# HGRN2 heads of a two-layer backbone: the context's state moved behind the sixth decay level, that level's scores in 32-wide strips

## The chip, the cores and the metric

The kernel runs on one core of a Trainium2 chip. Its engines work side by side, each with a queue of its own, in order: TensorE (PE for the matmuls, PEld for its weight loads), VectorE (DVE), ScalarE (ACT), GpSimd (POOL) and SyncE (SP, which here issues most loads). The metric is the device time of one execution in microseconds, the median of several; all times below are in us unless marked otherwise.

## The reference

Two layers act on 1024 latent tokens of width 1024 and a prefix of 256 context tokens. Layer 0 joins neighbourhood attention and a chunked mLSTM. Layer 1, which the change touches, is sixteen bidirectional HGRN2 heads (a gated linear recurrence), key and value width 128:

```
f = lb + (1 - lb) * sigmoid(f_pre)          # decay, per token and key channel, one per direction
S_t = diag(f_t) S_{t-1} + (1 - f_t) v_t^T   # state, 128 x 128
o_t = silu(q_t) S_t                         # both directions added
S_0 = state of the same recurrence over the 256 context tokens
y = rms_norm(o) * silu(z);  out = x + gate * (y @ w_out)
```

All is fp32. The context matters in layer 1 only through S_0: for each direction the sum over context tokens of v times k, k decayed by the product of all later f.

## The kernel before, in words

**Numbers.** A matmul of fp32 values is made of three matmuls of rounded halves: `dense` (L131 to L133) issues high x high, high x low and low x high for each 128-deep slice.

**Stages.** Layer 0 takes the time up to about 2165, with layer 1's first projections at its end (`hg_wide`, for the first head). Then come the sixteen heads, one every 60.3 us, until about 3110, then the output projection. Sixteen heads share one code path: `hg_intra`, `hg_close`, `hg_states`, `hg_chain`, `hg_scan`, and `hg_vt` and `hg_proj` for the next head.

**One head's scores.** The products q_t k_s with all decays between s and t are built in seven levels (`hg_level`): level `lev` pairs neighbouring blocks of 1 << lev tokens. K and Q hold keys and queries decayed to the border of their block, F (gF) the block's total decay. At each level ACT copies the keys of each left or right block side by side (ksel, L1467, one buffer), DVE multiplies K by the totals (L1462), PE multiplies ksel against Q in strips (L1431, 32 wide in levels 0 to 4, 64 wide in levels 5 and 6), DVE updates Q (L1462 again, same line), picks the strips into the diagonal blocks D (copy_predicated, L1491; levels 0 to 4) and halves the table of totals (L1489). Levels 5 and 6 are copied to the score matrix A (gA) by ACT (L1495, L1499). The strips of a level need the Q update of the level before and this level's ksel; ksel needs the K update of the level before.

**What PE does between levels.** `hg_vz` is a generator that gives the value and gate projections in eight pieces of 24 matmuls, 128x256 (2.65 us each); one piece runs after each level's strips, two after the last. After every second piece ACT copies the values out, makes a sigmoid, and DVE multiplies (gz, L1342).

**The context.** `hg_ctx` makes S_0: DVE scans the products of f over the context in both directions (L1354, L1355, into E, tile gEc), makes 1 - f (L1356) and the product k (L1357); PE transposes k (L1362, four), ACT copies it (L1365, tile gknc), PE multiplies it with the values (L1372, four), DVE copies the two states out (L1378). It is called at level 3, its second half at level 4.

**The previous head's tail.** `prev(1)` and `prev(2)` (called at levels 1 and 2) run `hg_out` for the first and second half of the previous head's tokens: PE transposes A (L1584), ACT scales it into gyt, of which there is one buffer (L1589), POOL issues a store to yd (L1590); from head 8 on POOL also issues transfers that add gyt to sums in memory (`s`, L1595: one for the first half, three for the second). `prev(3)`, called at level 4, runs `sums`: `wo_sums` loads four quarters of the output weight (L1558, into tiles gknc and gEc), makes four subtractions on POOL (L1559) and stores four results (`sw`, L1565); `y_diff` (only where the previous head is 1 to 8) loads two halves of a y (L1571, L1572, again gknc and gEc), subtracts (L1573) and stores (L1575). wo_sums runs where the previous head is 0 to 13, so in heads 1 to 14.

**What sets the order.** The code is written for one stream; a scheduler with a timing model of its own then places each instruction in its engine's queue by the code's order, the data dependencies and priorities. `urgent()` lowers a priority value by a million, so that what stands inside goes first; `seg()` pins PE's segments one behind another; `issue_after(x)` keeps an instruction behind x. Within a queue nothing overtakes. A tile tag with one buffer makes the next user wait for all readers of the last.

Of the kernel before, what the change touches and what calls it, by code (L numbers as in the profile page):

```python
# [14 lines left out]
ALU = mybir.AluOpType  # L15
# [4 lines left out]
P = 128  # L20
# [25 lines left out]
class Prog:  # L46
# [874 lines left out]
    def out_y(self, tt, q, ysrc, yp, bufs, raws=None, tag="y", ks=((0, 4), (4, 4)), late=None):  # L921
        pl, tg, nb = raws or (yp, "wraw", self.yraws)
        hi, lo = [], []
        for k, n in ks:
            yh = self.t(yp, [P, 512], F32R, tag + "h", bufs)
            yl = self.t(yp, [P, 512], F32R, tag + "l", bufs)
            k0 = q * 8 + k
            if callable(ysrc):
                yr = ysrc(k0, tt)
            else:  # L930
                yr = self.t(pl, [P, 512], F32, tg, nb)
                self.nc.sync.dma_start(
                    out=yr[:, 0 : n * P].rearrange("p (j t) -> p j t", j=n),
                    in_=ysrc[k0 : k0 + n, :, tt * P : (tt + 1) * P].rearrange("j p t -> p j t"),
                )
            m = self.split(yh[:, 0 : n * P], yl[:, 0 : n * P], yr[:, 0 : n * P])
# [156 lines left out]
    def hg_wide(self, sp, s1, tp, x, ctx_part, early):  # L1093
        nc, a = self.nc, self.a
# [100 lines left out]
        def unit(u, kind, i):  # L1195
# [60 lines left out]
            def P4():  # L1256
                t["d"] = self.ps("x", [P, 512])
                prod(t["d"], form("P4"), (1, 1), True)
                if u == end:
                    last_part()  # L1260
                    finish(1, 0, t["u3"])

            def P6():
# [27 lines left out]
            def P3():  # L1291
                w = form("P3")
                prod(t["c"], w, 4, False)
                add(t["u2"], t["c"], t["u2"])
                finish(0, 1, t["u2"])
                cpart(1, w, 4, True)

# [48 lines left out]
    def hg_ctx(self, st, pool):  # L1346
        nc = self.nc
        Fc, v = st["Fc"], st["v"]
        E = self.t(pool, [P, 2, CTX], F32, "gEc", 1)
        k = self.t(pool, [P, 2, CTX], F32, "gq", 2)  # L1350
        nc.vector.memset(E[:, 0, CTX - 1 : CTX], 1.0)
        nc.vector.memset(E[:, 1, 0:1], 1.0)
        zz = self.zero[:, 0 : CTX - 1]
        nc.vector.tensor_tensor_scan(E[:, 0, 0 : CTX - 1][:, ::-1], Fc[:, 0, 1:CTX][:, ::-1], zz, 1.0, ALU.mult, ALU.add)  # L1354
        nc.vector.tensor_tensor_scan(E[:, 1, 1:CTX], Fc[:, 1, 0 : CTX - 1], zz, 1.0, ALU.mult, ALU.add)  # L1355
        nc.vector.tensor_scalar(out=k, in0=Fc, scalar1=-1.0, scalar2=1.0, op0=ALU.mult, op1=ALU.add)  # L1356
        nc.vector.tensor_tensor(out=k, in0=k, in1=E, op=ALU.mult)  # L1357
        p = self.ps("tr", [P, 4, P])
        with self.seg():
            for d in range(2):  # L1360
                for j in range(2):
                    m = nc.tensor.transpose(p[:, 2 * d + j, :], k[:, d, j * P : (j + 1) * P], self.ident)  # L1362
        self.last_pe = m
        kn = self.t(pool, [P, 4, P], F32, "gknc", 1)
        nc.scalar.copy(kn, p)  # L1365
        yield
        S = []
        u = self.ps("s", [P, 2, P])
        with self.seg():
            for d in range(2):  # L1370
                for j in range(2):
                    m = nc.tensor.matmul(  # L1372
                        u[:, d, :], lhsT=kn[:, 2 * d + j, :], rhs=v[:, 8 + j, :], start=(j == 0), stop=(j == 1)
                    )
        self.last_pe = m
        for d in range(2):
            s = self.t(pool, [P, P], F32, f"gS{d}", 8)
            nc.vector.tensor_copy(s, u[:, d, :])  # L1378
            S.append(s)
        yield S  # L1380


    def hg_intra(self, h, st, pool, prev):
# [27 lines left out]
        for lev in range(7):  # L1411
            if lev == 5:
                hv["A"] = self.t(pool, [P, 8, P], F32, "gA", 1)
            self.hg_level(hv, lev, pool)
            if lev in (1, 2) and prev:
                prev(lev)
            if lev == 3:
                ctx = self.hg_ctx(st, pool)
                next(ctx)
            if lev == 4:  # L1420
                S = next(ctx)
                if prev:
                    prev(3)
            next(tiles)
        next(tiles)
        return hv, S


    def strip(self, out, b, n, lhsT, rhs):
# [19 lines left out]
    def hg_level(self, H, lev, pool):  # L1449
# [3 lines left out]
        K, Q, A, D, Tt = H["K"], H["Q"], H.get("A"), H["D"], H["T"]  # L1453

        pick = lambda t: _skew(t[:, 0, :].rearrange("p (b s i) -> p b s i", s=2, i=h), 2, n)
        w = 32 if lev < 5 else 64
        out = self.ps("s", [P, 8, w])

        def update(t, o, step):
            v = bass.AP(t.tensor, t.offset, [list(t.ap[0]), [n + h, 2], [2 * h, nb], [1, h]])  # L1460
            tot = bass.AP(Tt.tensor, Tt.offset + o, [list(Tt.ap[0]), [step, 2], [2, nb], [0, h]])
            nc.vector.tensor_tensor(out=v, in0=v, in1=tot, op=ALU.mult)  # L1462

        with self.urgent():
            if lev < 6:
# [5 lines left out]
            for c, b in ((c, b) for c in range(8) for b in range(P // w)):  # L1471
                with self.seg():
                    o = c * P + b * w
                    r = out[:, c, :]
                    if lev < 6:
                        r = r.rearrange("p (b s i) -> p b s i", s=2, i=h)
                        lhsT, rhs = ksel[:, o : o + w], pick(Q)[:, o // (2 * h) : (o + w) // (2 * h)]
                    else:
                        lhsT = K[:, b, o : o + 64]
                        rhs = Q[:, 1 - b, c * P + (1 - b) * 64 : c * P + (2 - b) * 64]  # L1480
                    run = self.strip(r, b, w, lhsT, rhs)
            self.last_pe = run
            update(Q, n + 1, -n - 1)
            if lev == 6:
                update(K, 1, n - 1)
            Tv = Tt[:, :, 0 : 2 * nb].rearrange("p d (b s) -> p d b s", s=2)
# [3 lines left out]
        if lev < 5:  # L1490
            nc.vector.copy_predicated(D, self.lmask[:, lev + 1, :].unsqueeze(1).to_broadcast([P, 8, 32]), out)  # L1491
            return
        for b in range(2):
            s, e = slice(b * 64, (b + 1) * 64), slice((1 - b) * 64, (2 - b) * 64)
            nc.scalar.copy(A[s, :, s if lev == 5 else e], out[s])  # L1495
        if lev == 5:
            for b in range(4):
                s = slice(b * 32, (b + 1) * 32)
                nc.scalar.copy(A[s, :, s], D[s])  # L1499

    def hg_states(self, st, H, d, c0, c1):
# [99 lines left out]
    def build(self):  # L1601
        tc, nc, a = self.tc, self.nc, self.a
        dma = nc.sync.dma_start
        with ExitStack() as es:
# [226 lines left out]
            with tc.tile_pool(name="op0", bufs=2) as op, ExitStack() as wl:  # L1831
# [58 lines left out]
            with l1:  # L1890
# [41 lines left out]
                self.hg_vt(0, st, pool, wv)  # L1932
                prev = None
                for h in range(16):
                    hv, (Sf, Sb) = self.hg_intra(h, st, pool, prev)
# [374 lines left out]
```

## Time and profile before

| what | us |
|---|---|
| median of three runs | 3284.87 (3284.54 to 3287.74) |
| the profiled execution | 3282.71 |
| its span, first to last instruction | 3280.7 |
| PE busy | 3213.6 (98%) |
| DVE / ACT / POOL busy | 2183.9 (67%) / 1481.6 (45%) / 797.8 (24%) |
| mean granted TensorE clock | 0.998 |
| level 2 to level 5 strips of head 4 (starts) | 2419.32, 2423.32, 2427.43, 2432.04 |

The profiled execution's own time lies 2.0 us above its span. In a timeline row the first number is the start from the span's beginning, the second the duration, then engine, line, operation, out<-in with shapes, and in brackets the idle time just before, with what ended it. Operations on one engine are pipelined, so a start can lie a little before the end of the row above. Line numbers are those of the kernel before; in the changed kernel the same lines stand 2 to 6 further down (L1356 is L1358 there, L1431 is L1434, L1462 is L1465, L1489 is L1495, L1589 is L1593).

### The profile page before, as it was taken

How to read it: one execution, taken by the hardware profiler on the slowest of the kernel's cores; microseconds unless marked ns; L12 is line 12 of the kernel's file. 1: busy time of each engine (PE TensorE's matmuls, PEld its weight loads, DVE VectorE, ACT ScalarE, POOL GpSimd, SP SyncE). 2: the span in 40 equal slices, each digit the busy share in tenths (PEclk: the TensorE clock that was granted, in tenths of full speed). 3: DMA queues.
4: the chain of work that ended last, by engine and by line, in shares of the span. 5: the costliest groups of instructions: out<-in, count | busy, mean ns of one | idle time of the engine just before them, and what ended most of it. 6: DMA issues, size and time to landing. Idle time of an engine off the chain costs nothing.

```text
span 3280.7 us, 70941 instructions
## 1 busy us (share of the span) xinstructions
PE 3213.6 (98%) x27818; PEld 2864.3 (87%) x27818; DVE 2183.9 (67%) x4993; ACT 1481.6 (45%) x3460; POOL 797.8 (24%) x1191
## 2 busy tenths in 40 slices
PE   7999999999999999999999999999999999999999
PEld 6799899988989888888878788889999999999977
DVE  5846666666655456678766855577767777667766
ACT  5245554455544434445446433344444444444443
POOL 2222222222211112211110133312323323334210
PEclk9999999999999999999999999999999999999999
DMA  7713322232233434445564233332232333434376
GB/s 246 255 50 86 87 72 82 69 94 85 67 92 101 149 102 128 138 122 163 175 194 129 87 100 103 106 99 63 97 118 85 103 106 99 103 95 102 95 219 169
DMA packets 338126, 380.20 MB, mean 116 GB/s; under 512 B 34600, under 2 KB 269800, under 8 KB 336768
## 3 DMA queue, kind: packets, MB, share of 16 engines
q1 hardware_dynamic: 286032, 236.73, 24.5%
q0 software_dynamic: 51760, 138.94, 13.6%
q8 instruction: 219, 3.59, 0.5%
q14 instruction: 115, 0.94, 0.1%
HBM read 272.31 MB, written 103.08 MB: 114 GB/s over the span
## 4 chain that ended last, share of the span: by engine, by line
PE 80%; DVE 7%; DMA 6%; issue 4%; ACT 2%; POOL 1%; SPq 1%; DVEq 0%; ACTq 0%; POOLq 0%
PE mm L131 15%; PE mm L132 15%; PE mm L133 15%; PE acc L889 3%; PE tr L869 2%; PE s L1431 2%; PE x L131 2%; PE x L132 2%; PE x L133 2%; PE mm L951 2%; PE mm L953 2%; PE mm L952 2%; PE acc L661 2%; PE s L670 2%; PE s L1506 1%
## 5 line engine op out<-in xcount | busy, mean ns | idle before, releaser
L131 PE MATMUL mm<-wh,hh 128*128 128x256 f32 (+1 forms) x1440 | 446.0, 310 | 2.7 <-ACT wh L73 0.7
L132 PE MATMUL mm<-wl,hh 128*128 128x256 f32 (+1 forms) x1440 | 445.3, 309 | 0.0
L133 PE MATMUL mm<-wh,hl 128*128 128x256 f32 (+1 forms) x1440 | 442.7, 308 | 0.0
L131 PE MATMUL mm<-hh,wh 128*128 128x512 f32 (+1 forms) x1076 | 391.3, 364 | 1.8 <-ACT ev L399 0.7
L132 PE MATMUL mm<-hl,wh 128*128 128x512 f32 (+1 forms) x1076 | 387.4, 360 | 0.7 <-DVE hl L346 0.7
L133 PE MATMUL mm<-hh,wl 128*128 128x512 f32 (+1 forms) x1076 | 386.8, 360 | 0.0
L131 PE MATMUL mm<-wzh,hh 128*128 128x256 f32 x1024 | 295.7, 289 | 0.0
L131 PEld LDWEIGHTS mm<-wh,hh 128*128 128x128 f32 x1440 | 271.7, 189 | 17.1 <-issue 1.0
L132 PE MATMUL mm<-wzl,hh 128*128 128x256 f32 x1024 | 285.1, 278 | 0.0
L133 PE MATMUL mm<-wzh,hl 128*128 128x256 f32 x1024 | 284.9, 278 | 0.0
L132 PEld LDWEIGHTS mm<-wl,hh 128*128 128x128 f32 x1440 | 271.6, 189 | 12.6 <-issue 0.7
L133 PEld LDWEIGHTS mm<-wh,hl 128*128 128x128 f32 x1440 | 271.4, 188 | 11.8 <-issue 0.5
L131 PEld LDWEIGHTS mm<-hh,wh 128*128 128x128 f32 x1076 | 202.9, 189 | 31.5 <-ACT ev L399 2.8
L133 PEld LDWEIGHTS mm<-hh,wl 128*128 128x128 f32 x1076 | 202.4, 188 | 29.5 <-issue 0.2
L132 PEld LDWEIGHTS mm<-hl,wh 128*128 128x128 f32 x1076 | 202.9, 189 | 28.4 <-DVE hl L346 1.4
L131 PEld LDWEIGHTS mm<-wzh,hh 128*128 128x128 f32 x1024 | 193.3, 189 | 2.3
L132 PEld LDWEIGHTS mm<-wzl,hh 128*128 128x128 f32 x1024 | 193.5, 189 | 0.0
L133 PEld LDWEIGHTS mm<-wzh,hl 128*128 128x128 f32 x1024 | 193.5, 189 | 0.0
L1462 DVE TENSOR_TENSOR gQ<-gQ,gF 128x1024 f32<-128x1024 f32 x112 | 145.1, 1295 | 20.0 <-PE s L1431 20.0
L1467 ACT COPY gksel<-gK 128x1024 f32<-128x1024 f32 x96 | 111.1, 1158 | 103.1 <-DVE gK L1462 98.1
L74 DVE TENSOR_TENSOR wl<-wraw,wh 128x512 fp32r<-128x512 f32 x174 | 118.4, 688 | 57.4 <-ACT wh L73 55.2
L1462 DVE TENSOR_TENSOR gK<-gK,gF 128x1024 f32<-128x1024 f32 x112 | 139.6, 1247 | 18.3 <-ACT gksel L1467 11.6
(608 smaller groups left out, 8477.7 us busy)
## 6 DMA issues: line engine op xcount, KB each, us to landing
wraw<-in_wab_dram SPq DMA_DIRECT2D x108, 256.0 KB
wraw<-yd SPq DMA_DIRECT2D x92, 256.0 KB
br<-in_wc_dram SPq DMA_DIRECT2D x66, 256.0 KB
md<-ev POOLq DMA_DIRECT2D x60, 256.0 KB, 2.7
wraw<-in_wc_dram SPq DMA_DIRECT2D x120, 128.0 KB
mloz<-md SPq DMA_DIRECT2D x40, 256.0 KB
s<-gyt POOLq DMA_DIRECT2D x36, 256.0 KB, 5.3
adar<-in_wada_dram SPq DMA_DIRECT2D x16, 512.0 KB
```

Of the source, the lines that this page charges most:

```text
L74: nc.vector.tensor_tensor(out=lo, in0=x, in1=hi.bitcast(F32), op=ALU.subtract)
L131: mm(ps, lhsT=lh(k), rhs=rh(k), start=(start and k == 0), stop=False, skip_group_check=skip)
L132: mm(ps, lhsT=lh(k), rhs=rl(k), start=False, stop=False, skip_group_check=skip)
L133: m = mm(ps, lhsT=ll(k), rhs=rh(k), start=False, stop=(stop and k == nk - 1), skip_group_check=skip)
L661: nc.tensor.matmul(num, lhsT=qc[:, j, :], rhs=C[d][:, j, :], start=False, stop=(j == 1))
L670: nc.tensor.matmul(u, lhsT=st["k"][c][:, j * P : (j + 1) * P], rhs=vw, start=True, stop=True)
L869: nc.tensor.transpose(pt[:nk, i, :], pr[:, o : o + nk], self.ident)
L889: m = nc.tensor.matmul(yp[h64], lhsT=v[:, h64], rhs=pTs[hd][:nk, i, :], start=(i == turn[0]), stop=(i == turn[-1]), tile_position=(0, hd * ...
L951: mm(ps, lhsT=yh[k], rhs=w.h(kk), start=(kk == 0), stop=False)
L952: mm(ps, lhsT=yh[k], rhs=w.l(kk), start=False, stop=False)
L1462: nc.vector.tensor_tensor(out=v, in0=v, in1=tot, op=ALU.mult)
L1467: m = nc.scalar.copy(ksel.rearrange("p (b s i) -> p b s i", s=2, i=h), pick(K))
```

## The change

1. `hg_ctx` yields ahead of its transposes. Its DVE part is called at level 5, placed behind that level's Q update; its PE part follows after level 6, between the last two value pieces, and the states are multiplied later, in the closing part (`Sf, Sb = next(ctx)` after the first projections of the next head).
2. Level 5's scores are 32 strips of 32x32 instead of 16 of 64x64: the strip takes Q from the plain tile instead of the picked one. ACT copies them in four pieces.
3. `prev(3)`, the sums, is called at level 2 and not at level 4.
4. Two seams: `last_part` and one addition at the end of `hg_wide` are made urgent; one weight block (`wf`) in layer 0's output part is kept behind a y block's split.

```
+            m = self.y_split = self.split(yh[:, 0 : n * P], yl[:, 0 : n * P], yr[:, 0 : n * P])
...
                 if u == end:
-                    last_part()
+                    with self.urgent():
+                        last_part()
...
-                add(t["u2"], t["c"], t["u2"])
+                with self.urgent() if u == end else ExitStack():
+                    add(t["u2"], t["c"], t["u2"])
...
         nc.vector.tensor_tensor(out=k, in0=k, in1=E, op=ALU.mult)
+        yield
         p = self.ps("tr", [P, 4, P])
...
-            if lev == 3:
+            if lev == 2 and prev:
+                prev(3)
+            if lev == 5:
                 ctx = self.hg_ctx(st, pool)
-                next(ctx)
-            if lev == 4:
-                S = next(ctx)
-                if prev:
-                    prev(3)
+                with self.tc.issue_after(self.level_q.ins):
+                    next(ctx)
             next(tiles)
+        next(ctx)
         next(tiles)
-        return hv, S
+        return hv, ctx
...
-        w = 32 if lev < 5 else 64
+        w = 32 if lev < 6 else 64
...
-                    if lev < 6:
+                    if lev < 5:
                         r = r.rearrange("p (b s i) -> p b s i", s=2, i=h)
                         lhsT, rhs = ksel[:, o : o + w], pick(Q)[:, o // (2 * h) : (o + w) // (2 * h)]
+                    elif lev == 5:
+                        o2 = c * P + (b ^ 1) * w
+                        lhsT, rhs = ksel[:, o : o + w], Q[:, 1 - b % 2, o2 : o2 + w]
...
-            update(Q, n + 1, -n - 1)
+            self.level_q = update(Q, n + 1, -n - 1)
...
-        for b in range(2):
-            s, e = slice(b * 64, (b + 1) * 64), slice((1 - b) * 64, (2 - b) * 64)
-            nc.scalar.copy(A[s, :, s if lev == 5 else e], out[s])
-        if lev == 5:
-            for b in range(4):
-                s = slice(b * 32, (b + 1) * 32)
+        for b in range(P // w):
+            s, e = slice(b * w, (b + 1) * w), slice((b ^ 1) * w, (b ^ 1) * w + w)
+            nc.scalar.copy(A[s, :, e], out[s])
+            if lev == 5:
                 nc.scalar.copy(A[s, :, s], D[s])
...
-                        wf = self.wring([a["wc"][:, 4096 : 4096 + P]], P)
+                        with tc.issue_after(self.y_split.ins):
+                            wf = self.wring([a["wc"][:, 4096 : 4096 + P]], P)
...
                     parts[0]()
+                    Sf, Sb = next(ctx)
                     self.hg_close(hv, 0, pool)
```

In the rows below a name such as gK is a tile's tag with its number. First DVE's queue in levels 0 and 1 of head 10, before:

```order
L1462 TENSOR_TENSOR gK_33216<-gK_33216,gF_32943 128x2x512
L1356 TENSOR_SCALAR gq_33518<-gFc_32944 128x512
L1406 TENSOR_TENSOR gD_33226<-s_33227,glm_4219_20262 128x256
L1462 TENSOR_TENSOR gQ_24883<-gQ_24883,gF_32943 128x2x512
L1491 COPY_PREDICATED gD_33226<-glm_4219_20262,s_33261 128x256
L1354 SCALAR_TENSOR_TENSOR gEc_33517<-gFc_32944,gzero_20260 128x255
L1355 SCALAR_TENSOR_TENSOR gEc_33517<-gFc_32944,gzero_20260 128x255
L1489 TENSOR_TENSOR gF_32943<-gF_32943 128x2x512
L1357 TENSOR_TENSOR gq_33518<-gq_33518,gEc_33517 128x512
L1462 TENSOR_TENSOR gK_33216<-gK_33216,gF_32943 128x2x256x2
L1462 TENSOR_TENSOR gQ_24883<-gQ_24883,gF_32943 128x2x256x2
```

and now:

```order
L1465 TENSOR_TENSOR gK_33396<-gK_33396,gF_33114 128x2x512
L1409 TENSOR_TENSOR gD_33406<-s_33407,glm_4219_20262 128x256
L1465 TENSOR_TENSOR gQ_24883<-gQ_24883,gF_33114 128x2x512
L1497 COPY_PREDICATED gD_33406<-glm_4219_20262,s_33441 128x256
L1495 TENSOR_TENSOR gF_33114<-gF_33114 128x2x512
L1465 TENSOR_TENSOR gK_33396<-gK_33396,gF_33114 128x2x256x2
L1465 TENSOR_TENSOR gQ_24883<-gQ_24883,gF_33114 128x2x256x2
```

The four context operations have left the stretch ahead of level 1's Q update (the last row of each). They now stand behind level 5's Q update (here of the head before, the changed kernel):

```order
L1465 TENSOR_TENSOR gQ_24883<-gQ_24883,gF_32254 128x2x16x32
L1353 MEMSET gEc_32997 128x1
L1354 MEMSET gEc_32997 128x1
L1356 SCALAR_TENSOR_TENSOR gEc_32997<-gFc_32255,gzero_20260 128x255
L1357 SCALAR_TENSOR_TENSOR gEc_32997<-gFc_32255,gzero_20260 128x255
L1358 TENSOR_SCALAR gq_32998<-gFc_32255 128x512
L1495 TENSOR_TENSOR gF_32254<-gF_32254 128x2x16
L1359 TENSOR_TENSOR gq_32998<-gq_32998,gEc_32997 128x512
L1495 TENSOR_TENSOR gT_33051<-gF_32254 128x16
L1344 TENSOR_TENSOR gz_32622<-gz_32622,mm_32925 128x256
L1465 TENSOR_TENSOR gQ_24883<-gQ_24883,gF_32254 128x2x8x64
L1465 TENSOR_TENSOR gK_32536<-gK_32536,gF_32254 128x2x8x64
```

Level 6's Q and K updates (the last two rows) follow them. Second POOL's queue at the start of head 10, from the end of the scan before it. Before:

```order
L1544 TENSOR_TENSOR gA_32812<-gA_32812,gss_32459 128x512
L1558 DMA gEc_33608<-in_woc_dram 128x256 x2
L1590 DMA yd_4_66<-gyt_33372 128x512
L1595 DMA s_13_75<-gyt_33372 128x512
L1590 DMA yd_4_66<-gyt_33447 128x512
L1595 DMA s_14_76<-gyt_33447 128x512
L1595 DMA s_15_77<-gyt_33447 128x512
L1595 DMA s_13_75<-gyt_33447 128x512
L1558 DMA gknc_33607<-in_woc_dram 128x256 x2
```

and now:

```order
L1548 TENSOR_TENSOR gA_32950<-gA_32950,gss_32621 128x512
L1562 DMA gEc_33634<-in_woc_dram 128x256 x2
L1563 TENSOR_TENSOR gknc_33633<-gEc_33634,gknc_33633 128x256
L1563 TENSOR_TENSOR gEc_33634<-gEc_33634,gknc_33633 128x256
L1569 DMA sw_17_79<-gknc_33633 128x256
L1563 TENSOR_TENSOR gEc_33634<-gEc_33634 128x256
L1569 DMA sw_18_80<-gEc_33634 128x256
L1594 DMA yd_4_66<-gyt_33552 128x512
L1599 DMA s_13_75<-gyt_33552 128x512
L1569 DMA sw_19_81<-gEc_33634 128x256
L1594 DMA yd_4_66<-gyt_33627 128x512
L1599 DMA s_14_76<-gyt_33627 128x512
```

The first y half's store and its adding transfer stood right behind the gEc loads; now three subtractions and two stores stand between. The gknc loads and the first subtraction have moved ahead of the scan, to the head before. Third PE's queue around the context's operations, the value pieces' matmuls left out. Before, at levels 3 to 5 of head 10:

```order
L1431 MATMUL s_33478<-gQ_24883,gksel_33479 32x32 x32
L1362 MATMUL tr_33525<-ident_82,gq_33518 128x128 x4
...
L1431 MATMUL s_33559<-gQ_24883,gksel_33560 32x32 x32
L1372 MATMUL s_33598<-gv_33184,gknc_33530 128x128 x4
```

and now, from level 5 on:

```order
L1434 MATMUL s_33803<-gQ_24883,gksel_33804 32x32 x32
...
L1434 MATMUL s_33884<-gQ_24883,gK_33396 64x64 x16
...
L1365 MATMUL tr_33932<-ident_82,gq_33850 128x128 x4
...
L1445 MATMUL tr_33986<-ident_82,gK_33396 128x128 x4
L1445 MATMUL tr_33993<-ident_82,gK_33396 128x128 x4
...
L1375 MATMUL s_34027<-gv_33364,gknc_33937 128x128 x4
L1445 MATMUL tr_34036<-ident_82,gK_33396 128x128 x4
```

The transposes left level 3 for the place between the last two value pieces, the state matmuls left level 4 for the closing part; level 5 has 32 strips.

More of the change, by code (lines that the diff above doesn't have):

```diff
@@ L935, in out_y @@
                 )
-            m = self.split(yh[:, 0 : n * P], yl[:, 0 : n * P], yr[:, 0 : n * P])
+            m = self.y_split = self.split(yh[:, 0 : n * P], yl[:, 0 : n * P], yr[:, 0 : n * P])
             if late:
@@ L1461, in update @@
             tot = bass.AP(Tt.tensor, Tt.offset + o, [list(Tt.ap[0]), [step, 2], [2, nb], [0, h]])
-            nc.vector.tensor_tensor(out=v, in0=v, in1=tot, op=ALU.mult)
+            return nc.vector.tensor_tensor(out=v, in0=v, in1=tot, op=ALU.mult)
         with self.urgent():
@@ L1934, in build @@
                 for h in range(16):
-                    hv, (Sf, Sb) = self.hg_intra(h, st, pool, prev)
+                    hv, ctx = self.hg_intra(h, st, pool, prev)
                     nxt, parts = self.hg_proj(h + 1, pool, None if h else self.hg_f(1, pool, wf)) if h < 15 else (None, [lambda: None] * 3)
```

## The prediction

> **What bounds the kernel now.** I read first the page's busy rows, then the waits of PE (TensorE's matmul queue) in the stretch of the sixteen heads, then the timelines of one head. The first row says that PE is the bound as a whole; its clock is full (0.998 over the span), so only idle gaps and issued work count.
>
> ```profile
> PE 3213.6 (98%) x27818; PEld 2864.3 (87%) x27818; DVE 2183.9 (67%) x4993; ACT 1481.6 (45%) x3460; POOL 797.8 (24%) x1191
> ```
>
> The second view lists what PE waited for between 2165 and 3150 us (in total, times, longest; the two entries below it are single waits outside this pattern):
>
> ```profile
> PE s L1431 <- DVE gQ L1462: 21.5, 16, 1.4
> ```
>
> Sixteen waits of 1.3 us: one per head, always for VectorE's (DVE's) update of Q. PE's timeline of the head at 2402 to 2464 us (h = 4) shows where:
>
> ```profile
> 2419.32 0.75 PE L1431 MATMUL s<-gQ,gksel 128*32 128x32 f32 x64 [1.44 <-DVE gQ L1462]
> 2423.32 0.76 PE L1431 MATMUL s<-gQ,gksel 128*32 128x32 f32 x64
> 2424.01 0.66 PE L1362 MATMUL tr<-ident,gq 128*128 128x128 f32 x4
> 2424.43 0.37 PE L131 MATMUL mm<-wzh,hh 128*128 128x256 f32 x1
> 2427.22 0.28 PE L133 MATMUL mm<-wzh,hl 128*128 128x256 f32 x1
> 2427.43 0.76 PE L1431 MATMUL s<-gQ,gksel 128*32 128x32 f32 x64
> 2428.12 1.16 PE L1372 MATMUL s<-gv,gknc 128*128 128x128 f32 x8
> 2429.04 0.36 PE L131 MATMUL mm<-wzh,hh 128*128 128x256 f32 x1
> 2432.04 1.15 PE L1431 MATMUL s<-gQ,gksel 128*64 128x64 f32 x32
> 2433.12 0.39 PE L131 MATMUL mm<-wzh,hh 128*128 128x256 f32 x1
> 2442.72 1.03 PE L1442 MATMUL tr<-ident,gK 128*128 128x128 f32 x8
> ```
>
> The wait is before level 2's strips. PE was ready at 2419.32 - 1.44 = 2417.88; levels 3, 4 and 5 follow without a gap. DVE's timeline of that head says why level 2 is late:
>
> ```profile
> 2410.92 1.27 DVE L1356 TENSOR_SCALAR gq<-gFc 128x512 f32<-128x512 f32 x1
> 2412.11 0.41 DVE L1406 TENSOR_TENSOR gD<-s,glm 128x256 f32<-128x256 f32 x1
> 2413.92 0.68 DVE L1354 TENSOR_TENSOR_SCAN gEc<-gFc,gzero 128x255 f32<-128x255 f32 x1
> 2415.10 1.19 DVE L1489 TENSOR_TENSOR gF<-gF 128x1024 f32<-128x1024 f32 x1
> 2416.22 0.68 DVE L1357 TENSOR_TENSOR gq<-gq,gEc 128x512 f32<-128x512 f32 x1
> 2416.82 1.21 DVE L1462 TENSOR_TENSOR gK<-gK,gF 128x1024 f32<-128x1024 f32 x1
> 2417.96 1.21 DVE L1462 TENSOR_TENSOR gQ<-gQ,gF 128x1024 f32<-128x1024 f32 x1
> 2421.68 1.22 DVE L1462 TENSOR_TENSOR gQ<-gQ,gF 128x1024 f32<-128x1024 f32 x1
> 2424.81 1.22 DVE L1462 TENSOR_TENSOR gQ<-gQ,gF 128x1024 f32<-128x1024 f32 x1
> 2433.24 1.50 DVE L1462 TENSOR_TENSOR gQ<-gQ,gF 128x1024 f32<-128x1024 f32 x1 [1.26 <-PE s L1431]
> 2436.87 0.42 DVE L1342 TENSOR_TENSOR gz<-gz,mm 128x256 f32<-128x256 f32 x1 [1.27 <-ACT gz L1341]
> ```
>
> The context work sits ahead of level 1's Q update: L1356 takes the queue for 2412.11 - 2410.92 = 1.19 us, the two scans for 2415.10 - 2413.92 = 1.18, L1357 for 2416.82 - 2416.22 = 0.60. Together 2.97 us.
>
> **Part 1, context work to level 5.** Without those 2.97 us the Q update that ended at 2419.17 ends at 2416.2, 1.7 us before PE is ready. I count the whole 21.5 us as gone. At its new place the work has room: level 5's Q update already waited 1.26 us for PE and the next gz 1.27 us for ScalarE (ACT). PE reaches level 5 earlier by 1.44 + 0.42 + 0.92 us (the wait, the transposes and the state matmuls that leave, by the starts above: 2424.43 - 2424.01 and 2429.04 - 2428.12), so level 5's strips end near 2429.9 and its Q update near 2431.2. The context's 3.0 us, two small T updates (0.8), gz (0.42), Q and K (1.21 each) bring DVE to 2437.8. PE wants the last K at its transposes L1442: 2442.72 less the 2.78 above, less 0.39 (part 2), plus 0.42 and 0.3 for the moved transposes, is 2440.3. The cover is 2.5 us; without it the excess would be paid 16 times.
>
> One wait is added there: the context's E shares a buffer (gEc) with POOL's difference of two y halves, which in heads 2 to 9 is loaded and read just before.
>
> ```profile
> gEc<-yd POOLq DMA_DIRECT2D x8, 256.0 KB, 3.9
> ```
>
> In head 4's time POOL's last store of the weight sums goes out near 2421 (part 3), the load follows its landing (2 us) near 2423.5, lands at 2427.4, and the subtraction, twice the 0.74 of one half as long (a row of part 3), ends at 2429: 2 us before E is wanted. If it came later, DVE's small T update, gz and level 6 would queue behind E, with the same 2.5 us of cover before PE notices. I take nothing.
>
> PE issues the same transposes and state matmuls as before, so their 0.42 and 0.92 us are moved, not saved. The state matmuls land beside other short work. The transposes, however, now split the last two value pieces, which ran as 48 matmuls without a break. A break costs the slower last start and first steps: 2427.43 - 2427.22 = 0.21 us before the strips where the stream's pitch is 0.11 to 0.12, 0.09 more in the first matmul (0.37 against 0.28), so 0.2 us; 24 matmuls with their borders against half of 48 give up to 0.38. I take 0.3: a loss of 16 x 0.3 = 4.8 us (3.2 to 6.1).
>
> **Part 2, level 5 in 32-wide strips.** The 64-wide strips hold PE for 2433.12 - 2432.04 = 1.08 us, the 32-wide ones of level 4 for 2428.12 - 2427.43 = 0.69. So 0.39 us a head, 16 x 0.39 = 6.2 us. ACT reads the result in four copies, not two:
>
> ```profile
> 2433.29 1.19 ACT L1495 COPY gA<-s 64x512 f32<-64x512 f32 x2 [4.01 <-PE s L1431]
> 2434.50 1.66 ACT L1499 COPY gA<-gD 32x256 f32<-32x256 f32 x4
> ```
>
> Four copies of 32x256 took 1.66 us against 1.19 for the two, 0.5 us more behind a 4 us idle: nothing.
>
> **Part 3, the sums of the output weights to level 2.** This is the part with a price. In heads 1 to 14 POOL (GpSimd) makes the previous head's weight sums; they move from behind level 4 to the head's start, and with them POOL's order. For heads 9 to 14 (previous head 8 or more) the first y half (gyt, one buffer) is also added to a sum in memory, and the second half cannot be written before that transfer has landed. In head 10:
>
> ```profile
> 2772.28 1.62 POOL L1544 TENSOR_TENSOR gA<-gA,gss 128x512 f32<-128x512 f32 x1
> 2779.50 1.17 POOL L1558 DMA_DIRECT2D gEc<-in_woc_dram  x2 [5.60 <-DVE gq L1357]
> 2780.66 0.54 POOL L1590 DMA_DIRECT2D yd<-gyt  x1
> 2781.20 0.94 POOL L1595 DMA_DIRECT2D s<-gyt  x1
> 2781.32 0.75 PE L1431 MATMUL s<-gQ,gksel 128*32 128x32 f32 x64 [1.42 <-DVE gQ L1462]
> 2786.94 0.69 ACT L1589 ACTIVATE gyt<-tr,hnc 128x512 f32<-128x512 f32 x1 [2.36 <-DMA s<-gyt]
> 2787.52 1.04 ACT L1467 COPY gksel<-gK 128x1024 f32<-128x1024 f32 x1
> 2789.99 0.76 PE L1431 MATMUL s<-gQ,gksel 128*32 128x32 f32 x64
> ```
>
> and all 28 adding transfers (the view by source line):
>
> ```profile
> DMA to landing us min/median/max: 4.0/5.6/7.8
> ```
>
> ACT waited 2.36 us for the transfer, and behind it in ACT's queue stood level 4's ksel, which ended at 2788.56, 1.4 us before PE used it. That slack is what part 1 removes: PE comes to level 4 earlier by the wait (1.42) and the transposes (0.42), at 2788.15. Now the transfer: POOL is free at 2773.9, issues the two loads until 2775.1 (they land 2.6 us after issue, near 2777.1), and before it may issue yd and s it now does three subtractions and two stores. Their durations are those of head 4:
>
> ```profile
> 2433.74 1.60 POOL L1559 TENSOR_TENSOR gknc<-gEc,gknc 128x256 f32<-128x256 f32 x1
> 2435.87 0.74 POOL L1559 TENSOR_TENSOR gEc<-gEc,gknc 128x256 f32<-128x256 f32 x1
> gEc<-in_woc_dram POOLq DMA_DIRECT2D x28, 128.0 KB, 2.6
> yd<-gyt POOLq DMA_DIRECT2D x30, 256.0 KB, 2.8
> ```
>
> Three times 0.74, two stores as long to issue as yd (0.54) and yd itself put the s issue at 2781.0 at best, as early as now; three times 1.60 put it at 2783.6. A subtraction took 1.60 where it met a DVE operation with both inputs in SBUF (Q at 2433.24 took 1.50, not 1.21, for the same meeting); at levels 1 to 3 DVE does little else, so I take 2782.5. The second gyt began 5.74 us after the issue in head 10, so it starts near 2788.2, ksel ends 1.62 us later at 2789.8, and PE, ready at 2788.15, waits 1.7 us. Bounds: 2781.0 with the shortest landing of 4.0 gives no wait; 2783.6 with 5.74 gives 2.8. Six heads: 6 x 1.7 = 10 us, from 0 to 17. In heads 1 to 8 only yd goes out of the first half. In head 4's time, 362.0 us before head 10's, it is issued between 2418.5 and 2421.1, lands 2.8 us later, and ksel is done 1.62 after that, by 2425.5 at the latest; PE comes to level 4 at 2427.43 - 1.44 - 0.42 = 2425.57: nothing.
>
> The Trainium skill (DMA: Bandwidth & Descriptors, section Anatomy of one DMA) gives about 2.0 us plus bytes over 436 GB/s, which for 256 KB is 2.6 us; yd's 2.8 agrees, the adding transfer's 5.6 does not, so the measured value is used. By the page's figure the wait in heads 9 to 14 would vanish and the clean case below would hold.
>
> **Part 4, the two seams.** In the order of instructions nothing stands differently on any engine before head 0's first context operation: nothing is gained or lost.
>
> **The sum.** -21.5 - 6.2 + 4.8 + 10 = -13 us. The profiled execution took 3282.71 (span 3280.7 and 2.0 around it), 2 us under the median of 3284.87; the difference is taken from the median: 3272.
>
> **Rivals.** *No new wait (clean).* If the adding transfer lands as early as now, heads 9 to 14 cost nothing: -22.9, 3262. For it: the best-case issue time equals today's. Against it: DVE is dense at levels 1 to 3, and two more stores stand in the same DMA queue.
>
> *The gain is eaten.* If those stores lengthen the landing to the 7.8 us that the slowest adding transfer took, 2.1 us more than 5.74, each of six heads waits 1.7 + 2.1 = 3.8: 23 us, and the sum is 0: 3285. For it: the row's spread of 4.0 to 7.8. Against: its median is 5.6.
>
> *Slower: DVE and POOL lock each other out in all heads.* Three subtractions now fall into levels 1 to 3 of heads 1 to 14. DVE's Q updates start 3.1 and 3.7 us apart there (2424.81 - 2421.68, 2421.68 - 2417.96) and PE's strips 4.0 and 3.7 (without the transposes), so DVE regains little. Level 2 has 1.7 us in hand. If each meeting cost a full 1.60 us instead of the 0.3 that Q lost at 2433.24, 4.8 us would come late, 3.1 beyond the slack: 14 x 3.1 = 43 us, less the 13 of the sum, is 30 more: 3315. It decides from a loss of 1.7 + 13 / 14 = 2.6 us a head, and makes it slower by over 0.2% from 1.7 + (13 + 6.6) / 14 = 3.1; there the time is 3292. Against it: three meetings of at most one subtraction (0.73) each are 2.2 us, 0.5 beyond the slack.
>
> The Trainium skill (SBUF — State Buffer, section Who interferes with whom) says that a DVE instruction with two SBUF inputs and a GpSimd one that reads SBUF exclude each other for a whole instruction. The trace agrees (1.50 and 1.60 above); by that rule this rival's loss is bounded by the subtraction's own length, which speaks against it, while it speaks for the later s issue.
>
> **Chances.** Forecast (heads 9 to 14 lose 1 to 3 us each: 3268 to 3280): 0.47, of which 0.07 falls within 0.2%. Clean: 0.24. Eaten: 0.17. Slower: 0.12. 0.2% is 6.6 us, about what a measurement of this kernel tells from no change. So faster 0.40 + 0.24 = 0.64, same 0.07 + 0.17 = 0.24, slower 0.12. The range starts at the clean case without any cost of breaks (21.5 + 6.2 off: 3257) and ends just past the eaten case, 3287.
>
> **What would show it.** Right: the wait for gQ at level 2 is gone from PE's list; strips of level 5 take 0.69 us; in its place stand about six waits of 1 to 3 us at level 4 for ksel (L1467), and ACT's gyt waits longer for s<-gyt. Wrong: fourteen or more waits for gQ or ksel, waits of PE for the moved transposes (the cover at levels 5 and 6 too thin), or waits at level 2 that remain.

## The result and the profile after

The changed kernel takes 3260.47 us, the median of four runs (3259.16 to 3262.34), against 3284.7 before in the same comparison: a ratio of 0.9926, with a 95% interval of 0.9909 to 0.9944. It is faster by 24 us, 0.74%. The forecast was 3272 in a range of 3257 to 3287: the sign and the range held, but the gain is nearly twice the 13 us of the sum, and the time lies below the band to which the forecast gave its own chance (3268 to 3280), close to the 3262 of the "clean" rival. That rival's mechanism is not what happened: the new waits that it left out are there.

The profiled execution took 3259.16 against 3282.71, 23.6 us less. From the first strips of head 0 to those of head 15 it took 885.5 us against 906.4, which is 20.9 of them; 1.5 came from head 15 and the rest behind it, 1.0 from the time at which head 0 began, 0.2 from outside the span.

The waits of PE in the stretch of the heads, after (total, times, longest):

```profile
PE s L1434 <- ACT gksel L1470: 3.2, 6, 0.7
PE s L1434 <- DVE p L1096: 2.3, 1, 2.3
PE s L1434 <- issue: 0.3, 1, 0.3
```

The sixteen waits for gQ, 21.5 us, are gone. (The prediction has one per head at level 2; in the timeline of before fifteen stood there, in heads 1 to 15, 1.29 to 1.44 us each, one of 0.40 stood at level 1 of head 13, and head 0 had none.) In their place stand six waits for ksel, as forecast, but of 0.4 to 0.7 us each and not 1.7. PE's timeline of head 4 (starts, us), after:

```profile
2406.30 0.77 PE L1434 MATMUL s<-gQ,gksel 128*32 128x32 f32 x64
2410.32 0.76 PE L1434 MATMUL s<-gQ,gksel 128*32 128x32 f32 x64
2414.53 0.75 PE L1434 MATMUL s<-gQ,gksel 128*32 128x32 f32 x64
2418.15 0.76 PE L1434 MATMUL s<-gQ,gksel 128*32 128x32 f32 x64
2421.77 0.76 PE L1434 MATMUL s<-gQ,gksel 128*32 128x32 f32 x64
2425.49 1.15 PE L1434 MATMUL s<-gQ,gK 128*64 128x64 f32 x32
2429.50 0.60 PE L1365 MATMUL tr<-ident,gq 128*128 128x128 f32 x4
2432.68 1.04 PE L1445 MATMUL tr<-ident,gK 128*128 128x128 f32 x8
```

and two rows of before that the prediction did not show:

```profile
2413.80 0.76 PE L1431 MATMUL s<-gQ,gksel 128*32 128x32 f32 x64
...
2436.07 1.15 PE L1431 MATMUL s<-gQ,gK 128*64 128x64 f32 x32
```

Shown are the strips of levels 1 to 6 (of before: levels 1 and 6). With the other rows of before one gets, level by level, what the head gained and lost. From level 1 to 2 it is 4.02 us now; before, it was 5.52 (2419.32 - 2413.80). From level 2 to 3 it is 4.21 against 4.00, from 3 to 4 it is 3.62 against 4.11, from 4 to 5 it is 3.62 against 4.61, from 5 to 6 it is 3.72 against 4.03. From level 6 to the first transposes of K it is 7.19 against 6.65, with the context's transposes now in between, and from there to the next head's level 0 strips 28.45 against 27.55, with the state matmuls now in between. So level 2 to 3 became slower by 0.2 us, although the view of waits names nothing there; the experiments say why.

### The profile page after: what moved, and what is told of

It is laid out like the page before. It is cut to its first block, busy times and chain, and to the rows that moved or that the text cites. A ratio compares the mean times of both kernels' runs of the same rounds, so it can differ in the third digit from the quotient of the medians.

```text
span 3257.4 us, 71990 instructions
## 1 busy us (share of the span) xinstructions
PE 3206.6 (98%) x28330; PEld 2855.2 (88%) x28330; DVE 2179.9 (67%) x4993; ACT 1486.3 (46%) x3492; POOL 810.9 (25%) x1191
## 3 DMA queue, kind: packets, MB, share of 16 engines
q1 hardware_dynamic: 286032, 236.73, 24.5%
## 4 chain that ended last, share of the span: by engine, by line
PE 81%; DMA 6%; DVE 6%; issue 4%; ACT 2%; POOL 1%; SPq 1%; DVEq 0%; ACTq 0%; POOLq 0%
PE mm L131 15%; PE mm L132 15%; PE mm L133 15%; PE acc L889 3%; PE tr L869 2%; PE s L1434 2%; PE x L131 2%; PE x L132 2%; PE x L133 2%; PE acc L661 2%; PE s L670 2%; PE mm L952 2%; PE mm L951 2%; PE mm L953 2%; PE s L1510 2%
## 5 line engine op out<-in xcount | busy, mean ns | idle before, releaser
L1465 DVE TENSOR_TENSOR gQ<-gQ,gF 128x1024 f32<-128x1024 f32 x112 | 152.9, 1366 | 0.9 <-PE s L1434 0.5
```

Source lines behind the costliest of these rows:

```text
L1465: return nc.vector.tensor_tensor(out=v, in0=v, in1=tot, op=ALU.mult)
```

## The experiments

Whole times of one program differ by several us from run to run, and head 0 began anywhere from 2166.6 to 2177.3 us in profiles of kernels whose instructions stand in one order up to there. So beside the medians I read the pitch of the heads in each profile, from a head's first strips to the next head's: the median over heads 1 to 8 and the mean over heads 9 to 14, in which the adding transfer matters. The median of before is that of the comparison with e1 to e4; e9 was executed once.

| kernel | median, us | heads 1 to 8 | heads 9 to 14 | head 0 to head 15 |
|---|---|---|---|---|
| before | 3284.4 | 60.41 | 60.63 | 906.4 |
| the change | 3260.5 | 58.78 | 59.56 | 885.5 |
| e1, sums behind the context | 3253.9 | 58.56 | 58.77 | 880.4 |
| e2, one more DVE operation | 3269.6 | 59.52 | 59.71 | 892.9 |
| e3, transposes at level 6 | 3265.9 | 59.11 | 59.65 | 889.8 |
| e4, level 5 in 64-wide strips | 3264.2 | 58.98 | 59.86 | 890.6 |
| e5, sums' move alone | 3389.9 | 69.16 | 67.69 | 1015.8 |
| e6, no seam edits | 3264.6 | 58.80 | 59.62 | 888.4 |
| e7, context's move alone | 3256.9 | 58.78 | 59.08 | 884.4 |
| e8, e1 again | 3258.3 | 58.56 | 58.79 | 880.4 |
| e9, e1 with loads ahead | 3264.5 | 58.56 | 60.51 | 890.4 |
| e10, the change again | 3259.0 | 58.61 | 59.42 | 884.7 |

**e1: are the six waits due to the place of the sums?**

```
-            if lev == 2 and prev:
-                prev(3)
...
         next(ctx)
+        if prev:
+            prev(3)
         next(tiles)
```

> The changed kernel, but the sums are called behind the context's transposes (after level 6) and not at level 2, so POOL issues the first y half's store and its adding transfer right behind the scan, as before the change. Theory (the six remaining waits at level 4 come from the sums that stand ahead of the adding transfer): the six waits for ksel, 3.2 us in all, vanish, and with them up to 0.5 us a head more in heads 9 to 14: about 3254 to 3258. Rival 1 (the adding transfer is late wherever it is issued): the six waits stay, 3260. Rival 2 (behind the context the sums and the y difference run into the next scan on POOL): PE or DVE waits for the scan's gss or for gA in heads 2 to 9, 1 us or more a head, 3265 or more.

3253.9 us (3249.74 to 3256.08), a ratio to before of 0.9904 (0.9888 to 0.9921). The waits of PE in the heads:

```profile
PE s L1434 <- DVE p L1096: 2.3, 1, 2.3
PE s L1510 <- ACT gkn L1447: 0.8, 2, 0.5
```

No wait for ksel is left; the one in the first row stands ahead of head 0. Heads 9 to 14 take 0.8 us less each than in the change, and heads 1 to 8 take 0.2 less: in head 4 the strips of levels 2 and 3 are 4.02 us apart again. Rival 1 and rival 2 fall. The theory's price was right for the six waits; that heads 1 to 8 gain as well it had not said.

**e2: how much slack has DVE?**

```
+            if lev == 1:
+                Te = Tt[:, :, 0 : 512]
+                nc.vector.tensor_scalar(out=Te, in0=Te, scalar1=1.0, scalar2=1.0, op0=ALU.mult, op1=ALU.mult)
             self.level_q = update(Q, n + 1, -n - 1)
```

> The changed kernel with one more DVE operation in every head: the totals F are multiplied by 1 in place (128x1024) ahead of level 1's Q update; the result is the same. It costs DVE an estimated 0.7 to 1.2 us. Theory of the trace after (DVE has only 0.2 to 0.4 us in hand at levels 2 and 3 of heads 1 to 14, since the sums' subtractions cost it about 1.5 us there): waits for gQ at level 2 or 3 come back, 0.3 to 1.0 us in each of 14 heads, 3265 to 3275. Rival (the prediction's 1.7 us of slack are still there): no waits, 3260.

3269.55 us, 9 more than the change, as the theory had it. From head 1 on PE's waits are

```profile
PE s L1434 <- DVE gQ L1465: 12.8, 17, 0.9
PE s L1434 <- issue: 0.5, 2, 0.3
```

and the operation itself took 0.90 us (median of 15). Of this, 0.74 us came through to PE (the heads' pitch rose from 58.78 to 59.52): level 1 to 2 became 0.93 us longer, and level 2 to 3 got back the 0.2 that it had lost. The prediction's slack of 1.7 us is not there, which the rows of POOL and DVE in head 4 of the change show:

```profile
2407.41 1.46 POOL L1563 TENSOR_TENSOR gknc<-gEc,gknc 128x256 f32<-128x256 f32 x1 [1.91 <-DMA gEc<-in_woc_dram]
2408.95 1.60 POOL L1563 TENSOR_TENSOR gEc<-gEc,gknc 128x256 f32<-128x256 f32 x1
2411.08 0.74 POOL L1563 TENSOR_TENSOR gEc<-gEc 128x256 f32<-128x256 f32 x1
```

```profile
2408.19 1.77 DVE L1465 TENSOR_TENSOR gQ<-gQ,gF 128x1024 f32<-128x1024 f32 x1
2410.21 0.90 DVE L1495 TENSOR_TENSOR gF<-gF 128x512 f32<-128x512 f32 x1
2411.21 1.71 DVE L1465 TENSOR_TENSOR gK<-gK,gF 128x1024 f32<-128x1024 f32 x1
2413.17 1.21 DVE L1465 TENSOR_TENSOR gQ<-gQ,gF 128x1024 f32<-128x1024 f32 x1
```

Three DVE operations took 0.56, 0.22 and 0.50 us longer than where POOL is quiet (1.21, 0.68, 1.21), 1.28 us together. What was in hand shows in head 4 of e1, where POOL makes no subtraction at these levels:

```profile
2410.05 1.22 DVE L1465 TENSOR_TENSOR gQ<-gQ,gF 128x1024 f32<-128x1024 f32 x1
2412.16 0.76 PE L1434 MATMUL s<-gQ,gksel 128*32 128x32 f32 x64
2413.78 1.22 DVE L1465 TENSOR_TENSOR gQ<-gQ,gF 128x1024 f32<-128x1024 f32 x1
2416.18 0.76 PE L1434 MATMUL s<-gQ,gksel 128*32 128x32 f32 x64
```

The Q updates end 0.89 us ahead of level 2's strips and 1.18 ahead of level 3's. Where PE waits for an update, its strips start 0.15 behind the update's end (before: 2419.17 and 2419.32). So DVE had about 0.75 us in hand at level 2 and 1.03 at level 3, and not 1.7. In the change level 2 keeps 0.2 of it (2409.96 against 2410.32). At level 3 the 1.28 us are more than the 1.03: level 2's Q update (last row of the change) ends at 2414.38 and level 3's strips start at 2414.53, right behind it. This is the hidden 0.2 us between levels 2 and 3, a wait too short for the list. Head 15 confirms the smaller slack: it has no subtractions, and in e2 it too waits at level 2, 0.23 us.

**e3: what does the break between the last value pieces cost?**

```
+            if lev == 6:
+                next(ctx)
             next(tiles)
-        next(ctx)
         next(tiles)
```

> The changed kernel, but the context's transposes stand right behind level 6's strips and not between the last two value pieces, so the last 48 value matmuls run without a break. Theory of the prediction (a break costs 0.3 us): 16 x 0.3 = 4.8 us faster, 3256. What the trace after suggests (0.13 us a head): 2 us faster, 3258. Rival (the product k is not ready there, it ended 0.5 us before that point): waits of PE for the transposes, 3260 or more.

3265.94 us, 5 more than the change; the rival has it. In the heads' stretch from head 1 on PE waited for

```profile
PE tr L1365 <- DVE gq L1359: 1.4, 5, 0.4
```

and the pitch of heads 1 to 8 rose by 0.3 us. In heads 3 to 7 k is not ready behind level 6's strips. Heads 10 to 15 show no such wait, and there level 6 to the transposes of K takes 7.05 us, against 7.19 in most heads of the change: without the break between the value pieces PE is 0.14 us faster, close to the 0.13 that the trace after had suggested.

**e4: what are the 32-wide strips worth?** The edit takes level 5 back to 16 strips of 64x64 and two copies of 64x512 on ACT.

> The changed kernel with level 5 back in 64-wide strips (16 of 64x64), all else kept. Theory (the strips' saving lies fully on PE's path): 0.39 us a head, 6.2 us slower than the change, 3266 to 3267. Rival (DVE or ACT is the bound at levels 5 and 6 now, so that shorter strips only move a wait): 3260 to 3262.

3264.18 us, 3.7 more than the change. In the profile level 5 to 6 of head 4 takes 4.02 us instead of 3.72, but 0.08 of that comes back in the next value piece, and the pitch rises by 0.20 us a head and not by 0.39. Between e7 (64-wide) and e1 (32-wide) it is 0.22. So by these pairs the strips are worth 0.2 us a head, 3 to 4 us in all; neither number was expected. The second execution of the change (e10) has a pitch of 58.61, and against it e4 loses 0.37: the price is known only to between 0.2 and 0.4.

**e5: the sums' move alone.**

```
+            if lev == 2 and prev:
+                prev(3)
             if lev == 3:
                 ctx = self.hg_ctx(st, pool)
                 next(ctx)
             if lev == 4:
                 S = next(ctx)
-                if prev:
-                    prev(3)
```

> The kernel before with one edit: the sums are called at level 2 and not at level 4; the context's work, its transposes behind level 3 and the 64-wide strips stay. In the order of instructions the context's scans and the product k then stand on DVE behind level 4's K update, because E shares gEc with the sums; only L1356 stays early. Theory (the parts hang together: without the context's move PE's transposes at level 3 wait for k, which comes only when POOL has read gEc): waits of PE for k at L1362 of 5 to 10 us in each of heads 1 to 14, the level 2 waits gone; 3340 to 3400. Rival (the sums' move is worth something by itself): the level 2 waits shrink and nothing takes their place, 3265 to 3280.

3389.92 us, a ratio of 1.032 (1.030 to 1.034). The waits of PE from head 1 on:

```profile
PE tr L1362 <- DVE gq L1357: 93.4, 14, 9.1
PE s L1431 <- ACT gyt L1589: 10.8, 14, 0.9
```

Fourteen waits of 6.7 us on the mean for k, as the theory had them. In heads 2 to 9 (7.3 to 9.1 us) E waits for gEc until POOL's difference of two y halves has read it: in head 4 this ends at 2450.26 and E's first scan starts at 2450.31. In heads 1 and 10 to 14 (3.1 to 5.7 us) the scans don't wait; k is late because they stand behind level 4's K update in DVE's queue. In one point the theory missed: the level 2 waits are not gone. The second row is theirs, put down to gyt, but in head 4 the strips start at 2439.84, 0.15 us behind the Q update's end. The sums can't go to level 2 without the context's move; whether the context could move with the sums left at level 4 no run shows, since e7 moves them as well.

**e6: the seams.** Both edits (urgent `last_part` and addition; `wf` behind the y split) are undone.

> The changed kernel with both seam edits undone. Its instructions stand on every engine in the same order as the changed kernel's. Theory (the seams do nothing): the changed kernel's time, 3258 to 3263, and the same six waits at level 4. Rival (they are worth what the start of head 0 showed, 1 us or more): 3264 or more.

3264.55 us (3259.47 to 3274.93 over six runs), by the letter in the rival's range. But the instructions stand in the change's order on every engine, the pitches are those of the change (58.80 and 59.62 against 58.78 and 59.56), and the six waits for ksel are there (3.5 us). What differs is where head 0 began (2171.1) and single heads, and the changed kernel itself began head 0 at 2167.5 once and at 2170.4 in e10. I take it as the measurement's spread: the seams do nothing that these runs can show.

**e7: the context's move alone.** From the kernel before, `hg_ctx` is called as in the change, with the sums behind it as in e1; the strips stay 64 wide and there are no seam edits.

> The kernel before with the context's move alone: its DVE part behind level 5's Q update, its transposes between the last value pieces, the sums kept behind it; level 5 in 64-wide strips, no seam edits. Theory (the removed level 2 waits are nearly the whole gain, a break costs next to nothing): 16 x 1.5 = 24 us less than before, 3259 to 3262, and no wait of PE in the heads over 0.5 us. By the prediction's price of a break (4.8 us) 3265 to 3268.

3256.91 us (3256.1 to 3259.94), below the theory's range. The pitch of heads 1 to 8 fell from 60.41 to 58.78, by 1.63 us, where the removed level 2 wait was 1.40 on the mean of fifteen heads and 1.44 in head 4. In all, the break costs nothing: in head 4 the transposes with the break cost 0.46 us where they now stand (7.11 against 6.65 from level 6 to K's transposes) and the state matmuls 0.90, and levels 3 to 5 without them are 1.49 shorter. One wait over 0.5 us is left that the theory did not allow: 0.69 for gkn in the closing part of head 13. The ratio to before, 0.9918 (0.9905 to 0.9931), is no worse than that of the whole change, 0.9926: what the strips bring, the sums at level 2 take back.

**e8: e1 once more**, beside e6 and e7.

> The kernel of e1 again (context's move, 32-wide strips, sums behind the context), beside the others on one chip and in five rounds: whether it beats the changed kernel. By e1: 6 us below e6, 3253 to 3256. If e1's lead was a draw of the measurement: the same as e6.

3258.27 us (3254.8 to 3262.61), 6.3 below e6 but 4 above e1. Its profile began head 0 at 2177.3, 9 us later than e1's, and then took the same 880.4 us to head 15. In the stretch that differs, the version with the sums behind the context is 4 to 5 us faster than the change, twice; in the whole time the lead is about as large as the spread of one program.

**e9: why was the adding transfer faster than before?** e1 with two extra loads of 128 KB ahead of it in heads 9 to 14:

```
...
+                pad = self.t(pool, [P, 512], F32, "gknc", 1)
+                nc.scalar.copy(pad.rearrange("p (k s) -> p k s", k=2)[:, :, 0], yt[:, 0:2])
+                for k in range(2):
+                    ld = nc.gpsimd.dma_start(
+                        out=pad[:, k * SQ : (k + 1) * SQ],
+                        in_=self.a["woc"][k * D : k * D + P, 0:SQ],
+                    )
...
```

Not shown are the condition on the head and the lines that keep the y store behind the loads and the adding transfer behind the store.

> The kernel of e1 with two extra loads of 128 KB in heads 9 to 14, issued by POOL right ahead of the first y half's store and its adding transfer, as the gEc loads stood in the kernel before; nobody reads what they load. It asks why the adding transfer landed 5.4 to 5.6 us after its issue in four of six heads before and 4.0 to 4.3 us in the changed kernel. Theory (loads still in flight ahead of it lengthen it): a landing of 5.0 us or more in most of heads 9 to 14. Rival (the loads have nothing to do with it): 3.9 to 4.8 us, as in e1.

One execution took 3264.45 us. The adding transfer landed 4.5, 4.9, 5.9, 4.5, 5.8 and 4.6 us after its issue in heads 9 to 14, 5.0 on the mean; before the change it was 4.7, 5.6, 5.6, 4.4, 5.4 and 5.5 (5.2), in the change 4.0, 4.1, 4.2, 4.1, 4.0 and 4.3 (4.1). "5.0 or more in most" was missed: two of six. In e1, with nothing but the y half's own store right ahead, it was 3.9 to 4.8, and in e8, the same kernel, 3.9 to 5.1 (4.3 on the mean in both). So the loads add 0.7 us on the mean. Values of 5.4 and more occur only with loads ahead (two of six here, four of six before, none of twenty-four in e1, e8 and the two executions of the change); the other four here overlap those of e1. PE's waits:

```profile
PE s L1434 <- ACT gksel L1470: 7.9, 6, 2.2
```

The wait at level 4 that e1 had removed is back, with up to 2.2 us (the loads also delay the issue by 1.2). Loads ahead can lengthen the transfer; why they do so in some heads and not in others stays open.

**e10: the change once more.**

> The changed kernel itself once more, to see how far one program's time and the stretch of its heads differ between executions. If the spread seen between kernels with one order of instructions (3260 and 3265) is the measurement's: 3258 to 3266, with the stretch from the first strips of head 0 to those of head 15 within 3 us of 885.5, and the six waits at level 4.

3259.04 us (3258.62 to 3260.88), 884.7 us from head 0 to head 15, six waits of 3.2 us in all, as expected. Its pitch in heads 1 to 8, 58.61, is 0.17 us below that of the first execution, nearly all of it behind level 5 (in head 4 3.61 and 7.11 us from level 5 to K's transposes, against 3.72 and 7.19). So a difference of 0.2 us a head between two kernels is firm only where it shows at one place in every head, as that at level 3 does (4.2 us here too).

## Why the prediction was right, point by point

**The bound and part 1.** The 21.5 us of level 2 were PE's and came back whole: 1.50 us between the strips of levels 1 and 2 in head 4, 1.63 us a head with the context's move (e7). The cover at levels 5 and 6 held: PE waited for neither k nor K at its new places, and in head 4 K's last update ended at 2429.47, 3.2 us ahead of its transposes, where the forecast had 2.5. But it is thin for k: behind level 6's strips, 2.9 us earlier, k is late in heads 3 to 7 (e3).

One number of part 1 was wrong, though it did not decide: the 1.7 us by which DVE would come ahead of PE at level 2. Before, L1356 met the last operation of POOL's scan; now level 0's Q update does. Two rows of before, then three of the change:

```profile
2410.27 1.63 POOL L1544 TENSOR_TENSOR gA<-gA,gss 128x512 f32<-128x512 f32 x1
2412.44 1.21 DVE L1462 TENSOR_TENSOR gQ<-gQ,gF 128x1024 f32<-128x1024 f32 x1
```

```profile
2402.78 1.61 POOL L1548 TENSOR_TENSOR gA<-gA,gss 128x512 f32<-128x512 f32 x1
2403.74 1.73 DVE L1465 TENSOR_TENSOR gQ<-gQ,gF 128x1024 f32<-128x1024 f32 x1
2425.66 0.40 DVE L1358 TENSOR_SCALAR gq<-gFc 128x512 f32<-128x512 f32 x1
```

L1356 took 1.27 us beside the scan and takes 0.40 at its new place, while the Q update rose from 1.21 to 1.73. From level 0's K update to level 1's it is 4.78 us now against 7.04: 2.26 us were freed, not 2.97, and the Q update ends 0.9 us ahead of level 2's strips where POOL makes no subtractions (e1).

**The break, 4.8 us of loss.** This term was wrong: e7 shows no loss, with 1.63 us gained a head where the wait was 1.44 at most. The prediction counted the transposes' and state matmuls' 0.42 and 0.92 us as moved without change and charged 0.3 for the new break on top. In head 4 the break costs 7.19 - 6.65 - 0.42 = 0.12 (e3 gives 0.14), and the two that left saved 0.49 and 0.99 us between the strips, 0.14 more than their own time. The two cancel.

**Part 2, 6.2 us.** Right in sign, too large: 0.39 us was read from strips of level 4; in place it was 0.3, of which 0.2 stayed (e4; e7 against e1): 3 to 4 us. Against e10 it would be 0.37, near the forecast, so the size stays open between these.

**Part 3, 10 us of loss.** In heads 9 to 14 this came to half of what was forecast. Its mechanism was right in every link. PE's waits stand at level 4, in heads 9 to 14, for ksel, behind gyt, behind the adding transfer. Head 10 of the change:

```profile
2756.28 1.62 POOL L1548 TENSOR_TENSOR gA<-gA,gss 128x512 f32<-128x512 f32 x1
2766.35 0.94 POOL L1599 DMA_DIRECT2D s<-gyt  x1
```

```profile
2770.58 0.69 ACT L1593 ACTIVATE gyt<-tr,hnc 128x512 f32<-128x512 f32 x1 [3.01 <-DMA s<-gyt]
2771.17 1.03 ACT L1470 COPY gksel<-gK 128x1024 f32<-128x1024 f32 x1
```

```profile
2772.26 0.76 PE L1434 MATMUL s<-gQ,gksel 128*32 128x32 f32 x64 [0.54 <-ACT gksel L1470]
```

The transfer was issued 8.45 us after the scan's last POOL operation (2766.35 less 2757.90), where the prediction had 8.6. Mis-sized was the landing: gyt began 4.23 us after the issue, where I took the 5.74 of before. That number was head 10's alone; its landing was 5.6, and the mean of the six heads before was 5.2. The new order put stores and not two loads ahead of the transfer, and by e9 loads there lengthen it in some heads, by 0.7 us on the mean. I had looked at what delays the issue and carried the landing over as a constant. So gyt began 12.68 us after the scan and not 14.3; that 0.54 us of wait remained is because PE too came to level 4 earlier than forecast, 13.82 us after the scan and not 14.25. The waits sum to 3.2 us and the whole loss in heads 9 to 14 to about 0.8 us a head, 5 us, against 10. The Trainium skill (DMA: Bandwidth & Descriptors, section Anatomy of one DMA) has 2.6 us for 256 KB by its formula; no adding transfer in these profiles landed under 3.8, so the measurements decide against it for this kind.

**The slower rival.** DVE and POOL do lock each other out in heads 1 to 14. Three meetings cost DVE 1.28 us in head 4. At level 2 that stayed within what DVE had in hand; at level 3, with 1.03 us in hand, 0.2 us came to PE in each head, which e1 gives back. With 0.9 us more on DVE (e2) the loss is 9 us in all. The Trainium skill's rule (SBUF — State Buffer, section Who interferes with whom), by which a meeting costs at most the other's instruction, agrees: 0.56, 0.22 and 0.50 us, none over a subtraction's 0.74. The prediction's "0.5 beyond the slack" was near the 0.2 us that showed, partly by luck: it set 2.2 us of meetings against 1.7 us at level 2, and measured were 1.28 against 1.03 at level 3. The forecast's sum had left the loss at zero.

**The seams.** Nothing, by the order of instructions and by e6.

**The sum by measured terms.** Level 2's wait with the context's move gives 15 x 1.63 = 24.5 us (head 0 did not wait there), the strips 16 x 0.2 = 3; the sums take back 14 x 0.2 = 3 and, in heads 9 to 14, 6 x 0.6 = 3.5 more (0.79 between the change and e1 there, less the 0.2). That is 21 us, against 22.4 from head 0 on in the profiled execution (20.9 and 1.5) and 24 in the medians; the forecast had 13. The largest miss is the context's move: 24.5 us against 21.5 - 4.8 = 16.7, from the break and from the interruptions that left with the moved work. The sums cost 6.5 and not 10, and the strips brought 3 and not 6.2, so that these two misses cancel. The 1.0 us by which head 0 began earlier belongs to no edit that these runs could show.

## What to carry to other kernels

A term that rests on a transfer's landing needs the question what will stand ahead of it in the new order, as much as when it is issued. When work leaves a place where it interrupted a stream, the interruption leaves with it, so a new break elsewhere is not a cost to add. An operation that was slow because it met another engine frees less than its time when it leaves, since the next operation takes over the meeting. And a queue whose slack just suffices shows no wait in a list with a threshold: compare the starts of the same instructions from level to level.

## What the runs showed of the hardware that was not expected

An adding transfer of 256 KB landed 3.9 to 4.3 us after its issue behind stores (the change, two profiles), and 4.4 to 5.9 behind two loads of 128 KB that had just been issued (before, and e9). A DVE operation of 1.21 us took 1.71 to 1.77 beside a POOL operation, and removing one operation that met POOL's scan only handed the meeting to the next. Level 5 to 6 took 0.3 us longer with 16 strips of 64x64 than with 32 of 32x32, although the narrow ones are twice as many. And the time at which head 0 began differed by 10.7 us among profiles whose programs stand in one order up to there, which is nearly half of what the change gained.
